# Moving one inner product and five instruction orders in a float32 decoder layer

## The chip, the cores and the metric

The program runs on one core of a Trainium2 chip. The metric is device time in microseconds (us) of one execution. The core has TensorE (PE in the profile, with its weight loads as PEld), VectorE (DVE), ScalarE (ACT), GpSimd (POOL) and SyncE (SP), which here issues most DMAs. Each engine takes its instructions in order, so where an instruction waits, what is queued behind it on that engine waits too.

## The reference

One layer of a hybrid decoder over 1024 prompt tokens and 8 x 8 sample tokens (1088 columns in all), model width 1024, everything float32:

```
xn   = rmsnorm(x, norm1_g)
q, k, v, glu_a, glu_b, gate_a, gate_b = split(xn @ w_in)
A    = attention(q, k, v; window 128, sinks) @ w_o_attn
B    = silu(layernorm(conv31(glu_a * sigmoid(glu_b)))) @ w_pb
h    = x + (sigmoid(gate_a) * A + sigmoid(gate_b) * B) @ w_out
up   = rmsnorm(h, norm2_g) @ w_up                 # 1024 -> 2 x 2816
gate, val = split(conv3(up))
y    = h + (silu(gate) * val) @ w_down            # 2816 -> 1024
out  = rmsnorm(y, norm_f_g)
```

Caches for attention and for both convolutions are outputs too.

## The kernel before

Activations lie as 128 channels by up to 1088 tokens. A float32 product is made of three matmuls (`mm3`, lines 195 to 197): weights and activations are each split into a rounded high part, cast on ScalarE (`whi`, L176 and L230), and the low rest, subtracted on VectorE (`wlo`, L177 and L231). Results gather in PSUM banks taken in turn from two groups, `mm` and `aux`; a bank can be written again when VectorE or ScalarE has moved its result out, an *eviction*.

The program is recorded in Python order, and a scheduler then places each engine's instructions by priorities. `self.later(n)` lowers a priority, `tc.issue_after(x)` puts what is recorded inside behind x, and `self.plan` hands steps to an agenda that `tick` runs off after so many k-steps.

The stages that matter here, in order of time:

- **Attention projection** (`phase_y`, about 640 to 736 us): eight streams `("o", m)`. `stream` calls `weight(what, ahead)`, which splits the weight of this stream and `ahead` more. Beside it the layer norm of the convolution branch runs from the agenda: VectorE adds eight channel blocks (L563), PE takes their mean (L571).
- **Up projection** (`ffn_up`, to about 1385 us): for each of 22 blocks f, a pair of row blocks (gate and value) is worked in quarters by a scheme with fewer products, Strassen-like. `pair(f)` runs its products n = 0, 1, ... in the order of `seq`, each with two halves j; an eviction of product n is L1713 (an add into `st`) or L1748 (a copy). From f = 4 on, eight times, two neighbouring blocks share one product: a *first* pair (f even) and a *second* (f odd). The shared product is itself split into seven small *inner* products, J11, JT2, J21, JT1, J22, JT3, JT4, of six matmuls each, made by `joint`, while the others, 0 to 5, are the *outer* ones. `JOINT_AFTER` says after which outer product an inner one is made, and `names` in `plan_pair` in which order their weights are prepared. JT3 and JT4 belong to the second pair; JT4's result is added to the gate's `st` (L1703). When a pair's results are there, `finish` convolves them: a first tap on ScalarE (L1400), two steps on VectorE for each of gate and value (L1402), Silu (L1408).
- **Down projection** (`ffn_down`, from about 1385 us): four plain groups, `down(0)` to `down(3)`, and two products of the same kind as above, `product(0)` and `product(1)`. The weights of group 0 are loaded and split in the last pair of the up projection (f = 21, n = 4; a plain pair of seven outer products). `product(0)` multiplies weight tiles `aw` with operands 0 to 20, three for each of its seven products p; an operand's word `bw` is loaded on SP (`words`) and split by ScalarE and VectorE (`operand`). L1904 evicts into H. `hooks[(m, p)]` says what is recorded behind product p of row block m.
- **Final norm**: `down(3)` goes over three chunks of columns; `final` takes the mean of squares on PE (L1969), the root on ScalarE and the reciprocal on VectorE (`rstd`, L356 and L357), scales eight blocks (L1973) and stores them in pairs. `tail` makes the last 128 tokens once more with tokens on the partitions, in two halves of 512 columns, squares them with a sum (L1993), and scales both halves (L2001) when the sum of both is there.

For the first norm of the layer the kernel has another form of the factor: `norm1_factor` makes the mean of squares as single columns (L320), and `norm1_spread` spreads the reciprocal root over 128 partitions with two matmuls for each piece (L339).

## Time and profile before

| | |
|---|---|
| runs | 1646.35, 1645.01, 1646.2 us; median 1646.2 |
| profiled execution | 1644.67 us; its span 1642.8 us; granted TensorE clock 0.999 |
| TensorE busy | 1632.3 us (99%), 11534 matmul records |
| VectorE busy | 1400.3 us (85%), 2595 instructions |
| ScalarE busy | 879.8 us (54%), 1844 instructions |
| GpSimd busy | 282.4 us (17%) |
| DMA | 201.57 MB, mean 123 GB/s |

A row of the timeline has the start and the duration in us, engine, line, operation, output <- inputs, shapes and count, and in brackets the idle time of the engine before it with what ended it. A row of the waits has who waited, for whom, the total, how often, and the longest. A row of the windows has the stretch, its length, the busy time and count of each engine, the granted clock, the DMA engines' busy share and GB/s.

### The profile page before, as it was taken

What the parts mean: (1) busy time and instruction counts of PE and PEld (TensorE: products, weight loads), DVE (VectorE), ACT (ScalarE), POOL (GpSimd) and SP (SyncE); (2) the same over time, 40 slices, a digit from 0 to 9 for tenths busy, and PEclk for the clock granted to TensorE, in tenths of its full rate; (3) what the DMA queues carried; (4) which work ended last, traced back from release to release, by engine and by line L of the source; (5) the groups of instructions that cost most, each with busy time, mean ns of one, the idle gap of its engine ahead of it and who ended that gap; (6) DMA issues with size and microseconds to landing.
All of it is one profiled execution on the core that took longest, in us unless ns stands there. A gap on an engine that the chain in (4) does not pass through costs nothing. (4 is left out here: it accounts for less than half of the span.)

```text
span 1642.8 us, 30190 instructions
## 1 busy us (share of the span) xinstructions
PE 1632.3 (99%) x11534; PEld 1614.9 (98%) x11534; DVE 1400.3 (85%) x2595; ACT 879.8 (54%) x1844; POOL 282.4 (17%) x549
## 2 busy tenths in 40 slices
PE   9999999999999999999999999999999999999998
PEld 9999999999999999999999999999999999999997
DVE  7899979999979996788755999988888877979867
ACT  6424277774488754676532466555555555524322
POOL 0100111222011111111102432333333220000000
PEclk9999999999999999999999999999999999999999
DMA  6221222323121255548763632344444334766423
GB/s 211 85 58 54 64 74 58 106 85 112 44 68 44 91 181 192 184 158 224 189 229 103 201 119 78 118 117 114 115 113 113 96 111 136 256 162 162 110 62 109
DMA packets 104856, 201.57 MB, mean 123 GB/s; under 512 B 25992, under 2 KB 56712, under 8 KB 104696
## 3 DMA queue, kind: packets, MB, share of 16 engines
q1 hardware_dynamic: 81528, 131.60, 26.5%
q0 software_dynamic: 22752, 67.79, 13.8%
q8 instruction: 90, 1.47, 0.4%
q14 instruction: 54, 0.44, 0.1%
q10 hardware_dynamic: 432, 0.27, 0.1%
HBM read 137.55 MB, written 64.03 MB: 123 GB/s over the span
## 5 line engine op out<-in xcount | busy, mean ns | idle before, releaser
L195 PE MATMUL mm<-xh,whi 128*128 128x384 f32 (+1 forms) x904 | 301.2, 333 | 0.0
L196 PE MATMUL mm<-xl,whi 128*128 128x384 f32 (+1 forms) x904 | 295.3, 327 | 0.3 <-DVE xl L282 0.2
L197 PE MATMUL mm<-xh,wlo 128*128 128x384 f32 (+1 forms) x904 | 295.4, 327 | 0.0
L196 PEld LDWEIGHTS mm<-xl,whi 128*128 128x128 f32 x904 | 170.0, 188 | 1.7 <-DVE xl L282 0.9
L195 PEld LDWEIGHTS mm<-xh,whi 128*128 128x128 f32 x904 | 169.8, 188 | 0.7
L197 PEld LDWEIGHTS mm<-xh,wlo 128*128 128x128 f32 x904 | 169.7, 188 | 0.1
L1402 DVE SCALAR_TENSOR_TENSOR acc<-st,fc,acc 128x1104 f32<-128x1104 f32 x88 | 119.8, 1364 | 9.2 <-issue 5.8
L176 ACT CAST whi<-wraw 128x1024 fp32r<-128x1024 f32 (+1 forms) x62 | 59.5, 966 | 66.0 <-PE mm L196 51.7
L197 PE MATMUL mm<-th,wlo 128*128 128x272 f32 x320 | 92.4, 289 | 0.0
L196 PE MATMUL mm<-tl,wlo 128*128 128x272 f32 x320 | 92.3, 289 | 0.0
L195 PE MATMUL mm<-th,wlo 128*128 128x272 f32 x320 | 92.3, 289 | 0.0
L525 DVE SCALAR_TENSOR_TENSOR bt<-u,consts,bt 128x513 f32<-128x513 f32 x120 | 89.8, 749 | 0.7
L525 DVE SCALAR_TENSOR_TENSOR c<-sm,hsum,c 128x512 f32<-128x512 f32 x120 | 89.6, 747 | 0.7
L197 PE MATMUL mm<-mh,wlo 128*128 128x272 f32 (+4 forms) x304 | 89.2, 293 | 0.0
L1748 ACT COPY st<-mm 128x272 f32<-128x272 f32 (+2 forms) x132 | 44.0, 351 | 78.0 <-PE mm L197 78.0
L525 DVE SCALAR_TENSOR_TENSOR c<-u,consts,c 128x512 f32<-128x512 f32 x112 | 83.7, 747 | 0.6
L230 ACT CAST whi<-wraw 128x512 fp32r<-128x512 f32 x76 | 47.3, 623 | 55.9 <-DVE wraw L1598 24.9
L177 DVE TENSOR_TENSOR wlo<-wraw,whi 128x1024 fp32r<-128x1024 f32 (+1 forms) x62 | 69.0, 1117 | 7.0 <-ACT whi L176 6.7
L378 ACT ACTIVATE p<-p,nm 128x257 f32<-128x257 f32 (+1 forms) x128 | 62.3, 490 | 11.9 <-DVE nm L373 11.5
L230 ACT CAST wlo<-wraw 128x512 fp32r<-128x512 f32 x76 | 47.5, 625 | 36.2 <-PE mm L197 24.0
L231 DVE TENSOR_TENSOR whi<-wraw,whi 128x512 fp32r<-128x512 f32 x76 | 52.2, 687 | 16.0 <-ACT whi L230 16.0
L195 PE MATMUL aux<-mh,whi 128*128 128x272 f32 (+4 forms) x216 | 63.9, 296 | 0.0
(707 smaller groups left out, 5788.2 us busy)
## 6 DMA issues: line engine op xcount, KB each, us to landing
wraw<-wall SPq DMA_DIRECT2D x118, 512.0 KB, 3.8
bw<-d_b SPq DMA_DIRECT2D x42, 272.0 KB, 4.0
d_b<-gd POOLq DMA_DIRECT2D x36, 272.0 KB, 4.8
d_b<-acc POOLq DMA_DIRECT2D x24, 272.0 KB, 4.5
ar<-wdn SPq DMA_DIRECT2D x32, 192.0 KB, 3.9
d_g<-acc POOLq DMA_DIRECT2D x10, 544.0 KB, 4.1
ga<-d_ga SPq DMA_DIRECT2D x8, 544.0 KB, 5.1
ct<-d_c SPq DMA_DIRECT2D x8, 544.0 KB, 5.7
```

The lines of the kernel that those rows point to most:

```text
L176: self.cast = self.nc.scalar.copy(h[:, z], r[:, z]).ins
L177: self.nc.vector.tensor_tensor(l[:, z], r[:, z], h[:, z].bitcast(F32), ALU.subtract)
L195: mm(ps, wh, xh, start=first, stop=False, skip_group_check=more)
L196: mm(ps, wh, xl, start=False, stop=False, skip_group_check=more)
L197: self.last_mm = mm(ps, wl, xh, start=False, stop=last, skip_group_check=more).ins
L230: self.cast = self.nc.scalar.copy(h, src).ins
L231: self.low = self.nc.vector.tensor_tensor(l, src, h.bitcast(F32), ALU.subtract).ins
L378: nc.scalar.activation(pt[:, j, lo:width + 1], pt[:, j, lo:width + 1], AF.Exp, bias=nm[:, j:j + 1], scale=-1.0, accum_out=den[:, j:j + 1])
L525: mac = lambda o, x, w: nc.vector.scalar_tensor_tensor(o, x, w, o, ALU.mult, ALU.add)
L1402: nc.vector.scalar_tensor_tensor(acc, st[:, k:k + AW], fw(f, k), acc, ALU.mult, ALU.add)
L1748: (add if second and n == 0 and j == 1 else op)(d, r(banks[bank, j]))
```

## The change

Five edits, none of which alters a result beyond the rounding of the last norm's factor.

1. The inner product JT4 stands behind outer product 4 of the second pair in place of 1, in `JOINT_AFTER` and in `names`.
2. The attention projection's stream `("o", 6)` no longer splits the weight of `("o", 7)` ahead; the agenda does, behind the last add of the layer norm's sum.
3. The weights of group 0 of the down projection are still loaded before product 4 of f = 21, but split behind its eviction.
4. In `product(0)`, words 18 to 20 are loaded behind product 0 as before, and their operands split behind products 1, 2 and 3, one each.
5. For the last chunk of `down(3)`, `final` is not called. `tail` makes the factor with `norm1_factor` in two pieces of one column, spreads it by `spread` into PSUM behind the first weight block of the second half, and the eight scalings read it there. The last 128 tokens: the second half is multiplied by the gains on VectorE while its sum is made, scaled on ScalarE and stored from ScalarE's queue; the first is scaled on VectorE and stored from SP.

```diff
-JOINT_AFTER = ({1: "J11", 2: "JT2", 3: "J21", 4: "JT1", 5: "J22"}, {0: "JT3", 1: "JT4"})
+JOINT_AFTER = ({1: "J11", 2: "JT2", 3: "J21", 4: "JT1", 5: "J22"}, {0: "JT3", 4: "JT4"})
...
+LAST_WEIGHT = 153
+FACTOR_AFTER = 1
...
-PIECES = {384: 3, 320: 4}
+PIECES = {384: 3, 320: 4, 256: 2}
...
-            add(live["red"][:, y * n:y * n + n], part[:, 0, :], part[:, 1, :])
+            self.summed = add(live["red"][:, y * n:y * n + n], part[:, 0, :], part[:, 1, :]).ins
...
-            self.stream(("o", m), xa, ev)
+            self.stream(("o", m), xa, ev, ahead=0 if m == KT - 2 else 1)
+
+        def last_weight():
+            with tc.issue_after(self.summed):
+                self.w_split()
 
         for m in range(KT):
+            if m == KT - 2:
+                self.plan([(self.now + LAST_WEIGHT - m * 3 * KT, last_weight)])
             do_o(m)
...
-                names = ("0", "JT3", "1", "JT4", "2", "3", "4", "5")
+                names = ("0", "JT3", "1", "2", "3", "4", "JT4", "5")
...
                     for _ in self.groups[0]:
                         self.w_load()
-                        self.w_split()
...
-                        (add if second and n == 0 and j == 1 else op)(d, r(banks[bank, j]))
+                        self.evicted = (add if second and n == 0 and j == 1 else op)(d, r(banks[bank, j]))
+                if f == NF - 1 and n == 4:
+                    with tc.issue_after(self.evicted.ins):
+                        for _ in self.groups[0]:
+                            self.w_split()
...
-            if last:
+            if last and c < len(TAIL_CHUNKS) - 1:
                 self.final(H, ssq, o, w)
+        self.last_ssq = ssq
...
-        hooks = {(0, 0): each(first, range(15, 21)), (0, 6): [lambda: self.w_ahead(2)], (1, 3): each(gated, (16,)),
+        hooks = {(0, 0): each(first, range(15, 18)) + each(lambda i: words(0, i), range(18, 21)),
+                 (0, 1): each(first, (18,)), (0, 2): each(first, (19,)), (0, 3): each(first, (20,)),
+                 (0, 6): [lambda: self.w_ahead(2)], (1, 3): each(gated, (16,)),
...
+        y = self.t(ft, [P, DM], "acc")
+        o, n = TAIL_CHUNKS[-1]
+        live = self.norm1_factor(ft, 3, self.last_ssq, self.bank("aux"), n)
...
+                if x == 0 and f == FACTOR_AFTER:
+                    self.final_rows(H, self.spread(live, n), o, n)
...
+        nc.vector.tensor_tensor(y[:, cs], ps, grow[:, cs], ALU.mult)
         nc.scalar.activation(s[:, 3:4], s[:, 1:2], AF.Sqrt, bias=s[:, 2:3], scale=1.0 / DM)
         nc.vector.reciprocal(s[:, 3:4], s[:, 3:4])
-        y = self.t(ft, [P, DM], "acc")
-        for cs, ps in halves:
-            nc.vector.scalar_tensor_tensor(y[:, cs], ps, s[:, 3:4], grow[:, cs], ALU.mult, ALU.mult)
-            nc.sync.dma_start(self.a["o_yt"][:, cs], y[:, cs])
+        nc.scalar.activation(y[:, cs], y[:, cs], AF.Identity, scale=s[:, 3:4])
+        nc.scalar.dma_start(self.a["o_yt"][:, cs], y[:, cs])
+        cs, ps = halves[0]
+        nc.vector.scalar_tensor_tensor(y[:, cs], ps, s[:, 3:4], grow[:, cs], ALU.mult, ALU.mult)
+        nc.sync.dma_start(self.a["o_yt"][:, cs], y[:, cs])
```

`final_rows` is the loop of eight scalings and four stores that stood in `final`; `spread` is the matmul part of `norm1_spread`, and it writes the factor to columns 0 to 255 of its bank and returns them.

What the edits do to the engines' orders is seen at three places. The first is VectorE in a joint second pair, from product 4's first eviction (`mm_11575`) on. Its second half lies in `mm_11588`, the gate's rows in `st_11502` and its convolution in `acc_11780`. Before:

```order
L1713 TENSOR_TENSOR st_11568<-st_11568,mm_11575 128x272
L1598 TENSOR_TENSOR wraw_1357_11420<-wraw_1357_11420,wraw_1356_11418 128x512
L1402 SCALAR_TENSOR_TENSOR acc_11780<-st_11502,fc_10182,acc_11780 128x1104
L1713 TENSOR_TENSOR st_11568<-st_11568,mm_11588 128x208
L1713 TENSOR_TENSOR st_11568<-st_11568,mm_11588 128x8x8
L231 TENSOR_TENSOR wlo_1382_11749<-wraw_1357_11420,wlo_1382_11749 128x512
L1402 SCALAR_TENSOR_TENSOR acc_11780<-st_11502,fc_10182,acc_11780 128x1104
L1598 TENSOR_TENSOR wraw_1357_11420<-wraw_1356_11418,wraw_1357_11420 128x512
L1563 TENSOR_TENSOR wraw_1356_11418<-wraw_1356_11418,wraw_11679 128x256
L231 TENSOR_TENSOR whi_1389_11809<-wraw_1357_11420,whi_1389_11809 128x512
```

The same place now, where product 4's halves are `mm_11572` and `mm_11585`, JT4's bank is `mm_11365`, and L1725, L1715, L1414, L1610, L1575 and L233 are the lines that were L1713, L1703, L1402, L1598, L1563 and L231:

```order
L1725 TENSOR_TENSOR st_11565<-st_11565,mm_11572 128x272
L1610 TENSOR_TENSOR wraw_1357_11420<-wraw_1357_11420,wraw_1356_11418 128x512
L1725 TENSOR_TENSOR st_11565<-st_11565,mm_11585 128x208
L1725 TENSOR_TENSOR st_11565<-st_11565,mm_11585 128x8x8
L233 TENSOR_TENSOR wlo_1382_11749<-wraw_1357_11420,wlo_1382_11749 128x512
L1715 TENSOR_TENSOR st_11502<-st_11502,mm_11365 128x272
L1610 TENSOR_TENSOR wraw_1357_11420<-wraw_1356_11418,wraw_1357_11420 128x512
L1575 TENSOR_TENSOR wraw_1356_11418<-wraw_1356_11418,wraw_11672 128x256
L1414 SCALAR_TENSOR_TENSOR acc_11780<-st_11502,fc_10182,acc_11780 128x1104 x2
L233 TENSOR_TENSOR whi_1389_11809<-wraw_1357_11420,whi_1389_11809 128x512
L1414 SCALAR_TENSOR_TENSOR acc_11787<-st_11565,fc_10182,acc_11787 128x1104
```

JT4's add stands between product 4's evictions and the gate's convolution, and both steps of that convolution stand behind it.

The second place is VectorE in `product(0)`, where `bw_16452` is word 20 and `aw` a weight tile. Before:

```order
L231 TENSOR_TENSOR ml_1857_16444<-bw_16442,ml_1857_16444 128x544
L231 TENSOR_TENSOR mh_1859_16449<-bw_16447,mh_1859_16449 128x544
L1904 TENSOR_TENSOR H_15876<-H_15876,aux_16457 128x272
L1904 TENSOR_TENSOR H_15876<-H_15876,aux_16468 128x272
L231 TENSOR_TENSOR ml_1861_16454<-bw_16452,ml_1861_16454 128x544
L231 TENSOR_TENSOR aw_16479<-ar_1775_16005,aw_16479 128x3x128
L1904 TENSOR_TENSOR H_15876<-H_15876,mm_16411 128x272
L1904 TENSOR_TENSOR H_15876<-H_15876,mm_16422 128x272
```

Now (L1920 was L1904, and words 18, 19 and 20 are `bw_16442`, `bw_16444` and `bw_16446`):

```order
L1920 TENSOR_TENSOR H_15876<-H_15876,aux_16448 128x272
L233 TENSOR_TENSOR ml_1861_16470<-bw_16442,ml_1861_16470 128x544
L1920 TENSOR_TENSOR H_15876<-H_15876,aux_16459 128x272
L233 TENSOR_TENSOR aw_16473<-ar_1775_16005,aw_16473 128x3x128
L1920 TENSOR_TENSOR H_15876<-H_15876,mm_16411 128x272
L233 TENSOR_TENSOR mh_1863_16496<-bw_16444,mh_1863_16496 128x544
L1920 TENSOR_TENSOR H_15876<-H_15876,mm_16422 128x272
L233 TENSOR_TENSOR aw_16499<-ar_1776_16007,aw_16499 128x3x128
L233 TENSOR_TENSOR ml_1869_16530<-bw_16446,ml_1869_16530 128x544
```

The three words' splits stand between the evictions, and word 20's behind both evictions of the next `mm` pair.

The third is PE at the end of the program; `mm_18696` and `mm_18716` are the two halves of the last 128 tokens. Before:

```order
L1969 MATMUL aux_18679<-fssq_18544,mean_79 128x256
L195 MATMUL mm_18696<-mh_2106_18144,mh_2103_18117 128x512
L196 MATMUL mm_18696<-ml_2107_18145,mh_2103_18117 128x512
L197 MATMUL mm_18696<-mh_2106_18144,ml_2104_18118 128x512
L195 MATMUL mm_18716<-whi_2065_17881,mh_2078_17989 128x512
L196 MATMUL mm_18716<-wlo_2066_17882,mh_2078_17989 128x512
```

Now (L197 to L199 were L195 to L197, L322 was L320 and L340 was L339):

```order
L322 MATMUL aux_18681<-mean_79,fssq_18544 128x1 x2
L197 MATMUL mm_18691<-mh_2106_18144,mh_2103_18117 128x512
L198 MATMUL mm_18691<-ml_2107_18145,mh_2103_18117 128x512
L199 MATMUL mm_18691<-mh_2106_18144,ml_2104_18118 128x512
L197 MATMUL mm_18727<-whi_2065_17881,mh_2078_17989 128x512
L340 MATMUL aux_18681<-identr_80,rowsh_2166_18685 128x128
L340 MATMUL aux_18681<-identr_80,rowsl_2167_18686 128x128
L340 MATMUL aux_18681<-identr_80,rowsh_2166_18685 128x128
L340 MATMUL aux_18681<-identr_80,rowsl_2167_18686 128x128
L198 MATMUL mm_18727<-wlo_2066_17882,mh_2078_17989 128x512
```

One matmul of 256 columns has become two of one column, and four of 128 columns stand inside the second half.

More of the change, by code (lines that the diff above doesn't have):

```diff
@@ L312, in norm1_chain, with norm1_factor @@
         return last
-    def norm1_factor(self, pp, c, sq, ps):
+    def norm1_factor(self, pp, c, sq, ps, n=None):
         nc = self.nc
-        n = CHUNKS[c][1]
+        n = n or CHUNKS[c][1]
         m = PIECES[n]
@@ L328, in norm1_factor, with spread @@
         return ps, h, l
-    def norm1_spread(self, pp, c, live):
+    def spread(self, live, n):
         nc = self.nc
-        n = CHUNKS[c][1]
         m = PIECES[n]
@@ L340, in norm1_spread @@
                                  start=x is h, stop=x is l)
+        return ps[:, :n]
+    def norm1_spread(self, pp, c, live):
+        n = CHUNKS[c][1]
+        ps = self.spread(live, n)
         rstd = self.t(pp, [P, 384], f"rstd{min(c, 1)}")
-        nc.scalar.copy(rstd[:, :n], ps[:, :n])
+        self.nc.scalar.copy(rstd[:, :n], ps)
         return rstd
@@ L1970, in final, with final_rows @@
         self.rstd(ssq[:, :n], ps[:, :n])
+        self.final_rows(H, ssq[:, :n], o, n)
+    def final_rows(self, H, rstd, o, n):
+        nc = self.nc
         for k in range(KT):
             hs = H[:, k, o:o + n]
-            nc.vector.scalar_tensor_tensor(hs, hs, self.c("gf", k), ssq[:, :n], ALU.mult, ALU.mult)
+            nc.vector.scalar_tensor_tensor(hs, hs, self.c("gf", k), rstd, ALU.mult, ALU.mult)
             if k % 2:
```

## The prediction

> **What bounds the kernel now.** The page's first part comes first.
>
> ```profile
> span 1642.8 us, 30190 instructions
> PE 1632.3 (99%) x11534; PEld 1614.9 (98%) x11534; DVE 1400.3 (85%) x2595; ACT 879.8 (54%) x1844; POOL 282.4 (17%) x549
> ```
>
> TensorE is busy nearly all the time, so only two things can shorten the run: a place where its next matmul starts late, and the stretch behind its last one. The profiled execution took 1644.67 us, 1.9 us more than its span and 1.5 us under the median of the three runs, 1646.2 us. I sum on the profiled execution and carry the difference over to the median. A difference of 0.2% is 3.3 us here, about what a measurement of this kernel can tell from no change.
>
> Next, the view of the waits on PE, which says who makes matmuls late. These two rows name the engine and line that the change moves.
>
> ```profile
> PE mm L195 <- DVE H L1904: 1.0, 1, 1.0
> PE mm L195 <- DVE st L1713: 0.4, 1, 0.4
> ```
>
> They understate it, since modelled matmul ends hide short waits. The sizes are therefore read from the timeline, from start to start.
>
> **Part 1: JT4 between products 4 and 5.** Three stretches of the timeline, PE and VectorE at the first joint second pair, then PE at the last of eight (f = 4, 6 to 18):
>
> ```profile
> 1046.93 0.29 PE L195 MATMUL mm<-th,whi 128*128 128x272 f32 x1
> ...
> 1048.44 0.28 PE L195 MATMUL mm<-mh,wlo 128*128 128x272 f32 x1
> 1048.66 0.39 PE L195 MATMUL mm<-th,whi 128*128 128x272 f32 x1
> 1048.89 0.28 PE L196 MATMUL mm<-tl,whi 128*128 128x272 f32 x1
> ...
> 1046.83 1.36 DVE L1402 SCALAR_TENSOR_TENSOR acc<-st,fc,acc 128x1104 f32<-128x1104 f32 x1
> 1048.11 0.49 DVE L1713 TENSOR_TENSOR st<-st,mm 128x208 f32<-128x208 f32 x2
> ...
> 1340.60 0.28 PE L195 MATMUL mm<-mh,wlo 128*128 128x272 f32 x1
> 1340.82 0.39 PE L195 MATMUL mm<-th,whi 128*128 128x272 f32 x1
> 1341.05 0.29 PE L196 MATMUL mm<-tl,whi 128*128 128x272 f32 x1
> ```
>
> Twelve matmuls of product 5's first half run from 1046.93 to 1048.44, a pitch of 0.126 us. Its second half needs the bank of product 4's second half, which ended just before 1046.93, but the eviction L1713 stands behind a convolution step L1402 and starts at 1048.11. So the matmul after 1048.44 comes at 1048.66 instead of 1048.57, and the one after that 0.23 later instead of 0.126: 0.09 + 0.10 = 0.19 to 0.20 us. At 1340.60 it is the same 0.22 and 0.23. Eight times 0.195 is **1.56 us**.
>
> After, six matmuls of JT4 (6 x 0.126 = 0.76 us) stand between the two products and both L1402 of the gate stand behind the eviction, which can start when its matmuls end, near 1047.1. The wait is then over more than 1 us before it matters. JT4's matmuls are moved, not added: PE work 0. What is late next: ScalarE's first tap of the gate now waits for JT4's add, and the gate's two L1402 with it, so VectorE meets the next pair later. There the nearest deadline is JT2, whose matmul reuses the bank that VectorE clears of J11:
>
> ```profile
> 1058.16 0.43 DVE L1703 TENSOR_TENSOR st<-st,mm 128x272 f32<-128x272 f32 x1
> 1059.97 0.29 PE L195 MATMUL mm<-mh,s 128*128 128x272 f32 x1
> ```
>
> J11 is cleared at 1058.59, 1.38 us ahead. By laying the new order over these durations I find VectorE 0.5 to 0.7 us late there, which leaves about 0.7. On POOL a store changes places with a small operation; no queue that PE waits for is behind it. Bounds: -1.57 to 0, and above it the slower rival; I take -1.56.
>
> **Part 2: down projection's first weights behind product 4's eviction (f = 21).** Timeline of VectorE and PE:
>
> ```profile
> 1380.83 1.23 DVE L177 TENSOR_TENSOR ml<-wraw,mh 128x1024 fp32r<-128x1024 f32 x1 [3.07 <-ACT mh L176]
> 1383.11 0.50 DVE L1713 TENSOR_TENSOR st<-st,mm 128x208 f32<-128x208 f32 x2
> ...
> 1382.96 0.29 PE L197 MATMUL mm<-th,whi 128*128 128x272 f32 x1
> 1383.66 0.39 PE L195 MATMUL mm<-th,whi 128*128 128x272 f32 x1 [0.41 <-DVE st L1713]
> 1383.89 0.29 PE L196 MATMUL mm<-tl,whi 128*128 128x272 f32 x1
> ```
>
> VectorE stands 3.07 us before a weight split whose cast is late, with the eviction of a finished product behind it (f = 21 is no joint pair: its two last products lie between). PE loses 0.70 - 0.126 = 0.57 and then 0.23 - 0.126 = 0.10: **0.67 us**. After, the eviction goes first and the splits, at the same time as now, end no later and hold up nothing before the down projection, which has the twelve matmuls from 1383.66 on (1.5 us) ahead of it. I take -0.67; bounds -0.67 and 0.
>
> **Part 3: product(0)'s operands 18 to 20 split one at a time.** Timeline of VectorE and PE:
>
> ```profile
> 1441.55 0.72 DVE L231 TENSOR_TENSOR ml<-bw,ml 128x544 fp32r<-128x544 f32 x1 [1.65 <-ACT ml L230]
> 1442.66 0.78 DVE L1904 TENSOR_TENSOR H<-H,mm 128x272 f32<-128x272 f32 x2
> ...
> 1441.89 0.28 PE L197 MATMUL aux<-e,aw 128*128 128x272 f32 x1
> 1443.15 0.39 PE L195 MATMUL mm<-e,aw 128*128 128x272 f32 x1 [0.98 <-DVE H L1904]
> 1443.38 0.29 PE L196 MATMUL mm<-e,aw 128*128 128x272 f32 x1
> ```
>
> VectorE waits for word 20, and the eviction L1904 stands behind it. PE loses 1.26 - 0.126 = 1.13 and 0.23 - 0.126 = 0.10: **1.24 us**. After, that eviction and the next weight tile stand ahead of word 20's split. Operands 18 to 20 belong to the last of seven products, two products of 18 matmuls (2.3 us each) further on, so the split itself, no later than now, has room. On SP two loads change places. I take -1.24; bounds -1.24 and, if word 20 holds up the following eviction by as much, 0.
>
> **Part 4: attention projection's last weight.** Only VectorE's order changes: the split (o,7) stands behind the three layer-norm adds, not before. Timeline of PE:
>
> ```profile
> 719.11 0.34 PE L197 MATMUL mm<-q,wlo 128*128 128x384 f32 x1
> 719.29 0.62 PE L571 MATMUL aux<-sm,mean 128*128 128x272 f32 x2
> ```
>
> The matmul that needs the adds starts 0.18 us after its neighbour, the ordinary distance: the adds are just in time. Nothing is gained; the split is wanted only when (o,7) starts. I take 0; bounds 0 and, if it came late by its own length, 1.2 us (the 1.23 of part 2's L177).
>
> **Part 5: final norm and the end.** Four groups of rows: matmuls of one column and the spreading matmuls where the kernel uses them already (timeline, PE), the mean matmul that goes, the last operations, and the windows' rates of the stores.
>
> ```profile
> 24.64 0.72 PE L320 MATMUL aux<-mean,sq 128*128 128x1 f32 x6
> 25.23 0.42 PE L197 MATMUL aux<-xh,q 128*128 128x384 f32 x1
> ...
> 40.69 0.22 PE L339 MATMUL aux<-identr,rowsh 128*128 128x128 f32 x1
> 41.31 0.39 PE L195 MATMUL mm<-xh,whix 128*128 128x384 f32 x1
> ...
> 1631.29 0.59 PE L1969 MATMUL aux<-fssq,mean 128*128 128x256 f32 x2
> 1631.95 0.40 PE L196 MATMUL mm<-ml,mh 128*128 128x512 f32 x1
> 1632.18 0.39 PE L197 MATMUL mm<-mh,ml 128*128 128x512 f32 x1
> ...
> 1636.29 0.60 ACT L1993 ACTIVATE st<-mm 128x512 f32<-128x512 f32 x1 [2.60 <-PE mm L197]
> 1637.64 1.41 DVE L2001 SCALAR_TENSOR_TENSOR acc<-mm,tsum,grow 128x512 f32<-128x512 f32 x2
> 1638.41 1.00 SPq L2002 DMA_DIRECT2D o_yt<-acc  x2
> ...
> 1639.75:1640.00 0.25, 0.00 (x0) 0.00 (x0) 0.00 (x0) 0.00 (x0) 0.00 (x0) 1.00 1.04 385
> 1640.50:1640.75 0.25, 0.00 (x0) 0.00 (x0) 0.00 (x0) 0.00 (x0) 0.00 (x0) 0.50 0.63 230
> ```
>
> On PE, L1969 costs 0.66 from its start to the second matmul behind it, less one pitch of 0.23: 0.43 us go. Two pieces of one column are four passes at 0.59 / 6 = 0.098, 0.39, and about 0.1 of restart behind them as behind the other waits: +0.5. Spreading is four matmuls at 0.62 / 6 = 0.103, 0.41, and 0.05 to 0.1 behind: +0.5. PE's last matmul, the last Square (1636.29) and the last reciprocal come 0.5 to 0.6 later, for no work that the end waits for. The eight norm operations start earlier, which frees VectorE but moves no end.
>
> The trace charges 0.098 us for a one-column pass. The Trainium skill, "TensorE: Matmul & The Clock Gate", section "Wait — 56ns, not 53.3ns?", puts the floor of a small matmul at about 25 ns from start to start; by that, an estimate, the four would cost 0.1 and the sum would be 0.3 us lower. The measured row decides.
>
> What is won back: now the two halves are scaled one behind the other on VectorE, 0.7 each, and the second store leaves at 1639.05 (1637.64 + 1.41). After, ScalarE and VectorE scale a half each at once, and both leave together, 0.7 earlier less the 0.55 of PE: about 1638.85 to 1638.95. But they also transfer together. Now the second store's 262 KB (128 x 512 x 4 bytes) end by 1640.75, and at 385 GB/s they took 0.68, so the first byte moved 1.0 us after the issue. After: 1638.9 + 1.0 + 524 KB at 385 GB/s (1.36) = 1641.2, **+0.45 us**. Bounds: the stores do not slow each other and PE adds 0.1 only, -0.6; PE adds 0.7 and the rate is nearer 300 GB/s, +1.0.
>
> That one engine's queue does not hide the other's transfer is the Trainium skill's rule too ("DMA: Bandwidth & Descriptors", section "Issuing engines are not separate DMA queues": all issuers share the same 16 engines). It speaks against this edit. Without it the second store would end at 1638.9 + 1.0 + 0.68 = 1640.6, and part 5 would be -0.15. No run here has two stores in two queues at the end.
>
> **The sum.** -1.56 - 0.67 - 1.24 + 0 + 0.45 = -3.0 us. The profiled execution would go from 1644.7 to 1641.7, the median from 1646.2 to **1643.2 us**, -0.18%, just inside the 0.2%.
>
> **The rivals.**
> - *The end is no dearer.* One-column passes are cheap or the stores overlap; part 5 is about -0.2 and the sum -3.7: 1642.5. For it: the second store's wait behind the first half is real. Against it: the rows of L320. Chance 0.16.
> - *A wait takes the place of part 1.* VectorE is in order and 85% busy; the delayed taps make another eviction late by the same 0.2. Parts 2, 3 and 5 remain: -1.5, 1644.7. For it: the eight joint pairs leave VectorE hardly any idle time. Against it: the 0.7 us left at JT2. Chance 0.10.
> - *The delayed taps stop PE (slower).* The gate's two L1402, 1.28 from start to start, both land ahead of J11's clearing instead of half of one. VectorE is then 2.56 late against the 1.38 of room; PE waits 1.18 and restarts in 0.1, in eight pairs 10.2. With the -3.0 of the forecast that is +7.2: 1653.4 (a lateness of 1.38 is where it begins; 2.1 makes the whole slower by 0.2%). Chance 0.09.
> - *The change does not do it.* Word 20 or the late cast still stands ahead of an eviction (ScalarE's order is in part unchanged), part 3 and 2 give nothing and part 5 costs: -1.1, 1645.1. Chance 0.05.
>
> **How the numbers follow.** The forecast has 0.60. Its own range is 1642.3 to 1644.4, from part 5's bounds and half of part 1. The range 1641.0 to 1645.6 adds the first, second and last rivals and the scatter of the runs shown, 1645.01 to 1646.35; it leaves out the slower one and the corners. Faster by over 0.2% (under 1642.9): a little under half of the forecast, 0.28, and nearly all of the first rival, 0.15: 0.43. Slower by over 0.2%: 0.09. Within: the rest, 0.48.
>
> **What would show it.** Right: the PE rows after product 5's first half keep 0.126 us at all eight pairs, and the waits on DVE st and DVE H are gone from PE's list; no row of more than 0.05 us takes their place near JT2; the last Square starts 0.5 us later against the last matmul group than now; the two last stores are issued within 0.2 us of each other and end together. Wrong: new waits of PE on L1703's or L1402's successors in the pairs, a matmul waiting for a weight split at the start of the down projection or at (o,7), or an end that comes earlier than 1.7 us after the last store's issue.

## The result, and the profile after

The changed kernel takes 1642.44 us (median of 19 runs, 1641.55 to 1644.54), the kernel before, beside it, 1645.75 (19 runs, 1644.34 to 1648.72). The ratio is 0.9979, with a 95% interval of 0.9972 to 0.9986: 3.3 us faster. Forecast were 3.0 us, from 1646.2 to 1643.2. The profiled execution took 1641.73 us against 1644.67, 2.94 less; its span is the first line here, with the engines' line of the page below it:

```profile
span 1639.9 us, 30209 instructions
PE 1631.1 (99%) x11540; PEld 1615.2 (98%) x11540; DVE 1401.3 (85%) x2597; ACT 880.5 (54%) x1845; POOL 262.7 (16%) x549
```

The view of PE's waits has lost its rows for `H` and `st`; a new one of 0.3 has come (on L1178, near 757 us; the rows on `warm` and `pth` belong to the first stages and stood in the list of before too):

```profile
PE mm L662 <- DVE warm L655: 1.1, 1, 1.1
PE aux L429 <- ACT pth L232: 0.8, 1, 0.8
PE mm L197 <- DVE ml L1178: 0.3, 1, 0.3
```

**Part 1.** Timeline of the changed kernel at the first joint second pair, PE and then VectorE:

```profile
1047.33 0.29 PE L199 MATMUL mm<-ml,s 128*128 128x272 f32 x1
1047.46 0.29 PE L197 MATMUL mm<-th,whi 128*128 128x272 f32 x1
...
1048.85 0.29 PE L199 MATMUL mm<-th,whi 128*128 128x272 f32 x1
1048.97 0.29 PE L197 MATMUL mm<-th,whi 128*128 128x272 f32 x1
...
1060.31 0.29 PE L197 MATMUL mm<-mh,s 128*128 128x272 f32 x1
...
1046.89 0.50 DVE L1725 TENSOR_TENSOR st<-st,mm 128x208 f32<-128x208 f32 x2
...
1048.29 0.43 DVE L1715 TENSOR_TENSOR st<-st,mm 128x272 f32<-128x272 f32 x1
...
1050.15 2.77 DVE L1414 SCALAR_TENSOR_TENSOR acc<-st,fc,acc 128x1104 f32<-128x1104 f32 x2 [0.37 <-ACT acc L1412]
...
1058.28 0.43 DVE L1715 TENSOR_TENSOR st<-st,mm 128x272 f32<-128x272 f32 x1
```

The six matmuls of JT4 end at 1047.46, product 5's first half takes 12 times 0.126 from there, and its second half follows at 1048.97 without a wait. The eviction that had started at 1048.11 starts at 1046.89. J11 is cleared at 1058.71, 1.60 before JT2 needs its bank at 1060.31.

**Parts 2 and 3 (edits 3 and 4).** Timeline of PE and VectorE at f = 21 and in `product(0)`:

```profile
1381.99 0.29 PE L199 MATMUL mm<-th,whi 128*128 128x272 f32 x1
1382.12 0.29 PE L197 MATMUL mm<-th,whi 128*128 128x272 f32 x1
1382.25 0.29 PE L198 MATMUL mm<-tl,whi 128*128 128x272 f32 x1
...
1377.80 0.51 DVE L1725 TENSOR_TENSOR st<-st,mm 128x208 f32<-128x208 f32 x2 [1.00 <-PE mm L199]
1378.21 1.22 DVE L179 TENSOR_TENSOR whi<-wraw,wlo 128x1024 fp32r<-128x1024 f32 x1
...
1440.25 0.28 PE L199 MATMUL aux<-e,aw 128*128 128x272 f32 x1
1440.37 0.29 PE L197 MATMUL mm<-e,aw 128*128 128x272 f32 x1
1440.49 0.29 PE L198 MATMUL mm<-e,aw 128*128 128x272 f32 x1
...
1437.18 0.44 DVE L1920 TENSOR_TENSOR H<-H,mm 128x272 f32<-128x272 f32 x1
```

The steps of 0.70 and 0.23 at f = 21, and of 1.26 and 0.23 in `product(0)`, are all 0.12 to 0.13 now. The first eviction waits for PE alone; the second stands behind a weight tile's split and starts 3.2 before PE takes up that group of banks again (1437.18 and 1440.37). Both go ahead of the splits that had held them up.

**Part 5.** Timeline of the last operations, and the windows around the last stores of after and then of before (the last two columns are the DMA engines' busy share and GB/s):

```profile
1628.14 0.50 PE L322 MATMUL aux<-mean,fssq 128*128 128x1 f32 x4
...
1628.51 0.48 PE L197 MATMUL mm<-mh,mh 128*128 128x512 f32 x1
...
1633.68 0.60 ACT L2020 ACTIVATE st<-mm 128x512 f32<-128x512 f32 x1 [3.19 <-PE mm L199]
1634.40 0.69 DVE L2024 TENSOR_TENSOR acc<-mm,grow 128x512 f32<-128x512 f32 x1 [0.99 <-ACT st L2020]
1635.01 0.15 DVE L2026 RECIPROCAL tsum<-tsum 128x1 f32<-128x1 f32 x1
1635.20 0.72 ACT L2027 ACTIVATE acc<-acc,tsum 128x512 f32<-128x512 f32 x1 [0.50 <-DVE tsum L2026]
1635.20 0.75 DVE L2030 SCALAR_TENSOR_TENSOR acc<-mm,tsum,grow 128x512 f32<-128x512 f32 x1
1635.95 0.38 ACTq L2028 DMA_DIRECT2D o_yt<-acc  x1
1635.98 0.34 SPq L2031 DMA_DIRECT2D o_yt<-acc  x1
```

```profile
1636.00:1636.50 0.50, 0.00 (x0) 0.00 (x0) 0.00 (x0) 0.00 (x0) 0.00 (x0) 1.00 0.00 0
1636.50:1637.00 0.50, 0.00 (x0) 0.00 (x0) 0.00 (x0) 0.00 (x0) 0.00 (x0) 1.00 0.35 135
1637.00:1637.50 0.50, 0.00 (x0) 0.00 (x0) 0.00 (x0) 0.00 (x0) 0.00 (x0) 1.00 1.02 389
...
1638.00:1638.50 0.50, 0.00 (x0) 0.00 (x0) 0.00 (x0) 0.00 (x0) 0.00 (x0) 0.50 0.43 152
```

```profile
1638.50:1639.00 0.50, 0.00 (x0) 0.00 (x0) 0.50 (x1) 0.00 (x0) 0.00 (x0) 1.00 0.98 350
1639.00:1639.50 0.50, 0.00 (x0) 0.00 (x0) 0.04 (x1) 0.00 (x0) 0.00 (x0) 1.00 0.90 309
1639.50:1640.00 0.50, 0.00 (x0) 0.00 (x0) 0.00 (x0) 0.00 (x0) 0.00 (x0) 1.00 1.04 387
```

From the start of the mean of squares (1631.29 before, 1628.14 now) to the last Square it is 5.00 before and 5.54 now, and to the end of the span 11.51 and 11.76. Before, the DMA engines never rest: the last half's stores run straight behind those of the eight row blocks. Now they are idle or all but idle (a share of 0.06 and then 0.00) from 1635.25 to 1636.75, and then move both halves together. The spans are given to 0.1, so the times to the end are good to about 0.05.

### The profile page after: what moved, and what is told of

Its sections match the earlier page's. It is cut to its first block, busy times and chain, and to the rows that moved or that the text cites. A ratio compares the mean times of both kernels' runs of the same rounds, so it can differ in the third digit from the quotient of the medians.

```text
span 1639.9 us, 30209 instructions
## 1 busy us (share of the span) xinstructions
PE 1631.1 (99%) x11540; PEld 1615.2 (98%) x11540; DVE 1401.3 (85%) x2597; ACT 880.5 (54%) x1845; POOL 262.7 (16%) x549
## 4 chain that ended last, share of the span: by engine, by line
PE 87%; DVE 7%; ACT 3%; DMA 2%; issue 1%; ACTq 0%; SPq 0%; DVEq 0%; POOLq 0%
PE mm L197 20%; PE mm L198 20%; PE mm L199 20%; PE aux L199 6%; PE aux L198 6%; PE aux L197 6%; PE aux L417 1%; DVE c L531 1%; ACT ct L611 1%; PE aux L429 1%; PE aux L430 1%; PE aux L407 1%; PE aux L408 1%; DVE bt L531 1%; DMA ct<-d_c 1%
## 5 line engine op out<-in xcount | busy, mean ns | idle before, releaser
L197 PE MATMUL mm<-xh,whi 128*128 128x384 f32 (+1 forms) x904 | 301.3, 333 | 0.0
L199 PE MATMUL mm<-xh,wlo 128*128 128x384 f32 (+1 forms) x904 | 295.4, 327 | 0.0
L197 PEld LDWEIGHTS mm<-xh,whi 128*128 128x128 f32 x904 | 169.9, 188 | 0.7
L199 PEld LDWEIGHTS mm<-xh,wlo 128*128 128x128 f32 x904 | 169.7, 188 | 0.1
L1414 DVE SCALAR_TENSOR_TENSOR acc<-st,fc,acc 128x1104 f32<-128x1104 f32 x88 | 119.7, 1363 | 12.2 <-issue 6.7
L199 PE MATMUL mm<-th,wlo 128*128 128x272 f32 x320 | 92.4, 289 | 0.0
L197 PE MATMUL mm<-th,wlo 128*128 128x272 f32 x320 | 92.4, 289 | 0.0
L199 PE MATMUL mm<-mh,wlo 128*128 128x272 f32 (+4 forms) x304 | 89.2, 293 | 0.0
L1412 ACT ACTIVATE acc<-st,fc 128x1104 f32<-128x1104 f32 x44 | 57.6, 1314 | 14.5 <-DVE st L1715 11.9
L197 PE MATMUL aux<-mh,whi 128*128 128x272 f32 (+4 forms) x216 | 63.9, 296 | 0.0
```

Of the source, the lines that this page charges most:

```text
L197: mm(ps, wh, xh, start=first, stop=False, skip_group_check=more)
L199: self.last_mm = mm(ps, wl, xh, start=False, stop=last, skip_group_check=more).ins
L1412: nc.scalar.activation(acc, st[:, 0:AW], AF.Identity, bias=fb(f), scale=fw(f, 0))
L1414: nc.vector.scalar_tensor_tensor(acc, st[:, k:k + AW], fw(f, k), acc, ALU.mult, ALU.add)
```

## The experiments

Times of runs of one kernel scatter by some 2 to 4 us, so the parts are read from the traces: the start of the same matmul on PE is compared with the kernel before, and a stretch of the program is worth what this difference grows by. Edit 2 acts between 700 and 740 us; the joint pairs are edit 1, f = 21 is edit 3, the words are edit 4. The last column is the time from the mean of squares to the end of the span.

| run | us | 700 to 740 | 740 to 762 | joint pairs | f = 21 | words | tail |
|---|---|---|---|---|---|---|---|
| before | 1644.67 | | | | | | 11.51 |
| after | 1641.73 | +0.03 | +0.71 | -1.50 | -0.67 | -1.24 | 11.76 |
| jt4_last | 1642.05 | +0.10 | +0.35 | -1.50 | -0.67 | -1.24 | 11.78 |
| jt4_three | 1643.01 | +1.48 | +0.42 | -1.64 | -0.68 | -1.24 | 11.73 |
| jt4_two | 1643.51 | +1.36 | +0.21 | -0.94 | -0.67 | -1.24 | 11.76 |
| only_last_weight | 1646.26 | +1.51 | +0.27 | +0.02 | +0.75 | -1.00 | 11.53 |
| split_and_words | 1642.63 | +0.24 | +0.37 | -0.02 | -0.67 | -1.24 | 11.49 |
| old_mean_new_halves | 1641.08 | +0.02 | +0.30 | -1.50 | -0.67 | -1.24 | 11.66 |
| new_mean_old_halves | 1643.01 | +1.11 | +0.34 | -1.49 | -0.67 | -1.24 | 11.48 |
| one_queue | 1641.90 | +0.13 | +0.37 | -1.50 | -0.67 | -1.24 | 11.75 |
| quarters | 1641.78 | +0.03 | +0.03 | -1.50 | -0.67 | -1.24 | 12.65 |
| end_alone | 1645.52 | +1.62 | +0.55 | 0.00 | -0.02 | -1.12 | 11.96 |

All are single profiled executions. One loss is in no column: new_mean_old_halves loses 0.73 more near 955 us, where PE waits for a weight split (L1463), and no other kernel does. The runs fall into three groups.

**JT4's place (part 1).** The first two kernels move JT4 on from its new place, the third goes between old and new.

```diff
-JOINT_AFTER = (..., {0: "JT3", 4: "JT4"})
+JOINT_AFTER = (..., {0: "JT3", 5: "JT4"})   # jt4_last
+JOINT_AFTER = (..., {0: "JT3", 3: "JT4"})   # jt4_three
+JOINT_AFTER = (..., {0: "JT3", 2: "JT4"})   # jt4_two
```

(`names` follows.) For jt4_last the expectation was:

> The changed kernel with JT4 behind outer product 5 instead of 4: no inner product stands between products 4 and 5 any more, but VectorE's order keeps both L1402 steps of the gate behind product 4's eviction. Theory (the wait of 0.19 us in each joint second pair came from the convolution step ahead of the eviction): the eviction starts near the end of product 4, a good 1 us before its bank is wanted, so the eight waits stay away and the stretch of the joint pairs is within 0.2 us of the changed kernel. Rival (JT4's 0.76 us of matmuls between the products are what covers the wait): 0.09 + 0.10 us come back at each of eight pairs, +1.5 us. A second rival: JT4's bank comes free later and the next pair's first matmuls wait, up to 0.5 us a pair, +4 us.

It came out so: -1.50 and no wait in the eight pairs, with no matmuls of JT4 between products 4 and 5. The cover is not needed. For jt4_three:

> The changed kernel with JT4 behind outer product 3 instead of 4: JT4 is still moved away from product 1, and one step of the gate's convolution stands ahead of product 4's second eviction again, as in the kernel before. Theory (VectorE's order decides): the eight waits are back with about 0.19 us each, the stretch of the joint pairs is 1.5 us longer than in the changed kernel. Rival (it is enough that JT4 is later than product 1): no waits, the stretch as in the changed kernel.

This failed. One step of the convolution does stand ahead of the eviction, and yet the stretch gives -1.64. Timeline of VectorE in before, where JT4's add is the first row, and in jt4_three, where it is the L1715:

```profile
1039.10 0.43 DVE L1703 TENSOR_TENSOR st<-st,mm 128x272 f32<-128x272 f32 x1
...
1045.27 0.69 DVE L231 TENSOR_TENSOR whi<-wraw,whi 128x512 fp32r<-128x512 f32 x1 [0.40 <-ACT whi L230]
```

```profile
1046.25 0.43 DVE L1715 TENSOR_TENSOR st<-st,mm 128x272 f32<-128x272 f32 x1
1046.74 0.69 DVE L233 TENSOR_TENSOR whi<-wraw,whi 128x512 fp32r<-128x512 f32 x1
...
1048.42 1.36 DVE L1414 SCALAR_TENSOR_TENSOR acc<-st,fc,acc 128x1104 f32<-128x1104 f32 x1
1049.70 0.50 DVE L1725 TENSOR_TENSOR st<-st,mm 128x208 f32<-128x208 f32 x2
```

PE is 1.97 later in jt4_three at this place (most of it its loss near 720 us, below). Counted from PE, the split of `whi` starts at 1044.77 there and at 1045.27 before, and the eviction at 1047.73 and 1048.11. In before JT4's add stands in a stretch in which VectorE has next to no idle time, and then VectorE idles 0.40 for a cast. In jt4_three the add stands in that idle time, the cast and all behind it come earlier, and the eviction is 0.38 earlier, twice the 0.19 that PE lost. So a third theory: not what stands directly ahead of the eviction, but how late VectorE is when it gets there, and behind product 2 the add should still make it late:

> JT4 behind outer product 2, the rest as in the changed kernel. Theory: VectorE works without a gap for 12 us ahead of the late eviction, up to an idle stretch of 0.40 us where it waits for a cast; JT4's add (0.43) makes the eviction late as long as it stands in that full stretch. Behind product 2 it still does, so the 0.19 at each of eight pairs comes back: the joint stretch changes by 0 against before and the run is 1.5 slower than the changed kernel. If any place later than product 1 were enough, the stretch shows -1.5 as with JT4 behind product 3.

```profile
1043.32 0.43 DVE L1715 TENSOR_TENSOR st<-st,mm 128x272 f32<-128x272 f32 x1
...
1046.92 0.69 DVE L233 TENSOR_TENSOR whi<-wraw,whi 128x512 fp32r<-128x512 f32 x1 [0.40 <-ACT whi L232]
...
1049.76 0.50 DVE L1725 TENSOR_TENSOR st<-st,mm 128x208 f32<-128x208 f32 x2
```

Half right. The idle 0.40 is back and so is a part of the wait, but only a part: -0.94 instead of 0 and instead of -1.5. Counted from PE (1.74 later here) the eviction starts at 1048.02, 0.09 earlier than before. The eight pairs are not alike: in the first six PE still loses 0.10 each (no wait is left, only the slow step of 0.23 instead of 0.126 behind it), in the last two nothing. Together, counted from the eviction's start to the matmul that takes its bank: 0.46 before (to where that matmul would stand without the wait), with a loss of 0.19 a pair; 0.55 in those six pairs, with 0.10; 0.68 in the last two, 0.65 to 0.95 in jt4_three, 1.31 in jt4_last and 2.08 in the changed kernel, with none. The lateness sets the price, about tenth for tenth; the changed kernel wins 1.6 where 0.2 were enough.

**Edits 2 to 4.** Edit 2 alone, and edits 3 and 4 alone, on the kernel before:

```diff
+            self.stream(("o", m), xa, ev, ahead=0 if m == KT - 2 else 1)   # only_last_weight
...
+                    with tc.issue_after(self.evicted.ins):                  # split_and_words
+                        for _ in self.groups[0]:
+                            self.w_split()
```

> The kernel before with the edit of the attention projection's last weight alone. In the profile of the changed kernel the stretch from 740 to 760 us took 0.72 us longer than before, with a cast waiting 1.2 us for a weight load instead of 0.7. Theory (chance of one load's landing, the edit is neutral): the stretch is within 0.3 us of the kernel before, and where it is not, the load was issued at the same time and landed later; the whole is 1644 to 1646. Rival (the weight load that the moved split releases goes out 2.4 us later and pushes the later loads): the same +0.5 to +0.8 us again, and a new wait of PE on DVE ml near 757.

> The kernel before with two edits alone: the down projection's first weights split behind product 4's eviction at f = 21, and operands 18 to 20 of product(0) split one by one. Theory: PE's waits on DVE st near 1383 and on DVE H near 1442 are gone and nothing takes their place, -0.67 and -1.24 us, together -1.9 us against the kernel before. Rival (ScalarE's order is partly unchanged, so a late cast holds up another eviction): half of it or less, with a new wait of PE within 10 us behind either place.

The second came out to the hundredth: -0.67 and -1.24, and no new wait. The first came out between 740 and 762 us (+0.27), but showed +1.51 near 720 us, where PE waits for the layer norm's sum. That looked like a cost of edit 2, but the end alone, whose program is that of before up to the last 20 us, has it too:

```profile
720.47 0.73 PE L577 MATMUL aux<-sm,mean 128*128 128x272 f32 x2 [1.33 <-DVE sm L569]
```

> The new end alone, on the kernel before. The tail from the mean of squares to the end is 11.76, 0.25 longer than before, with the last Square at 5.54; the joint stretch, f = 21 and the words change by 0, and no wait of PE near 720 or 760 us is new: about 1645.9 beside 1645.7.

Of the eleven profiled executions with edit 2 (those of the table, and old_end and serial_quarters below) four lose 1.1 to 1.5 us there, of the three without it one. It is scatter of a load: VectorE's work on the second half of that layer norm's input waits for a DMA, first in before, then in end_alone:

```profile
698.17 0.72 DVE L563 TENSOR_TENSOR u<-ct 128x544 f32<-128x544 f32 x1 [0.87 <-DMA ct<-d_c]
```

```profile
699.47 0.73 DVE L569 TENSOR_TENSOR u<-ct 128x544 f32<-128x544 f32 x1 [2.06 <-DMA ct<-d_c]
```

That load took 7.0 to 7.2 us from issue to landing in the five executions with the loss and 5.5 to 5.8 in the other nine. The norm's later steps carry the delay on: ScalarE's Square (L596) starts at 717.52 in end_alone against 716.22 in before (L590). Why the load lands late was not settled. The 0.03 to 0.71 near 750 us are taken for scatter as well: a cast there waits 0.17 to 1.25 for a weight load in all runs, and the runs without edit 2 show 0.37 and 0.55. Edit 2 itself does bring the sum forward: its last add starts 2.38 behind that Square in all eleven executions with the edit and 2.60 in all three without. These 0.22 count only where PE waits for the sum; between before and after they did not.

The last column but one holds one more thing. In the two runs that came 1.8 late from 720 us without edit 4, the wait for word 20 was nearly gone (-1.12 and -1.00): the word landed 0.7 and 1.7 later than before, while PE came to it 1.84 and 2.70 later. A loss ahead of such a wait can be paid back by it, but need not be: in only_last_weight the wait at f = 21 grew by 0.75, since its weight load was issued 1.8 later, as PE was, but landed 2.5 later.

**The end (part 5).** Four kernels are the changed one with a piece of its end undone or altered:

```diff
-            if last and c < len(TAIL_CHUNKS) - 1:
+            if last:                     # old_mean_new_halves: factor and scalings as before
...
+        for cs, ps in halves:            # new_mean_old_halves: halves one behind the other, as before
+            nc.vector.scalar_tensor_tensor(y[:, cs], ps, s[:, 3:4], grow[:, cs], ALU.mult, ALU.mult)
+            nc.sync.dma_start(self.a["o_yt"][:, cs], y[:, cs])
...
-        nc.scalar.dma_start(self.a["o_yt"][:, cs], y[:, cs])
+        nc.sync.dma_start(self.a["o_yt"][:, cs], y[:, cs])      # one_queue
...
+        for x in range(2):               # quarters: each half in two pieces of 256 columns
```

> The changed kernel with the last chunk's factor made as before (mean matmul, root and reciprocal of 128 x 256 in SBUF), the last 128 tokens as changed. Times are counted from the start of the mean's matmul (1631.29 before, 1628.14 changed): before, the last Square comes at 5.00, the second store at 7.78, the end of the span at 11.51; changed, 5.54, 7.84, 11.76. Theory (one-column and spreading matmuls cost PE 0.5; VectorE is then the bound, since its eight scalings end at 6.2 as before and the multiply stands behind them): Square at 5.0, stores at 7.6 to 7.7, end 11.5 to 11.7. Rival (the new form's 0.5 us of PE is all there is to it): everything behind the Square 0.54 earlier, stores at 7.3, end at 11.2.

> The changed kernel with the last 128 tokens scaled and stored as before (both halves on VectorE one behind the other, both stores from SP), the factor as changed. From the start of the mean's matmul, as in the run beside it. Theory: Square at 5.54, reciprocal right behind the root at 6.6, stores at 7.6 and 8.3, end 3.73 behind the second, 12.0: 0.25 us worse than changed, 0.5 worse than before. Rival (two stores that leave together share the engines so that nothing is won by leaving together): end 11.7 to 11.8 as changed.

> The changed kernel with the second half's store issued from SP too, in front of the first half's. Theory (all stores share the same 16 engines, and the end is set by 524 KB behind the first byte): the first store leaves as now, the second one issue of 0.34 us later, both end within 0.15 us of the changed kernel (11.76 from the mean's matmul to the end of the span). Rival (two queues move more than one): the end is 0.3 us or more later.

> The changed kernel with each half of the last 128 tokens scaled and stored in two pieces of 256 columns, two on ScalarE, two on VectorE, so that the first bytes can move about 0.35 us earlier. Theory (behind the last scaling the stores' transfer bounds the end): first stores at 7.45 instead of 7.82 from the mean's matmul, the last at 7.9, end 11.4 to 11.5, 0.3 us earlier than changed. Rival (the end is bound by the time from the last issue to the landing, 3.9 us): end 11.8 or later.

old_mean_new_halves came out as expected (Square 5.00, stores 7.64 and 7.67, end 11.66). The other three follow the table.

| kernel | last Square | stores issued | bytes move from about | tail |
|---|---|---|---|---|
| before | 5.00 | 7.13, 7.79 | without a pause | 11.51 |
| after | 5.54 | 7.80, 7.83 | 8.7 | 11.76 |
| old_mean_new_halves | 5.00 | 7.64, 7.67 | 8.5 | 11.66 |
| new_mean_old_halves | 5.52 | 7.55, 8.21 | 8.4 | 11.48 |
| one_queue | 5.54 | 7.80, 8.24 | 8.6 | 11.75 |
| quarters | 5.51 | 7.54, 7.57, 8.02, 9.73 | 8.4 | 12.65 |

Times are in us from the mean of squares. new_mean_old_halves went against its expectation of 12.0: with the second store leaving 0.4 later than in after, the end is 0.28 earlier. Its windows show why:

```profile
1638.00:1638.50 0.50, 0.00 (x0) 0.00 (x0) 0.00 (x0) 0.00 (x0) 0.00 (x0) 1.00 0.76 291
1638.50:1639.00 0.50, 0.00 (x0) 0.00 (x0) 0.00 (x0) 0.00 (x0) 0.00 (x0) 1.00 1.05 385
1639.00:1639.50 0.50, 0.00 (x0) 0.00 (x0) 0.00 (x0) 0.00 (x0) 0.00 (x0) 0.94 0.94 365
```

The transfer of one half (0.68) is as long as the scaling of one (0.66 from start to start), so two halves one behind the other keep the DMA engines full from the first store on. What counts between these two is when the first half leaves: 7.55 there, 7.80 in after. one_queue gave 11.75, as expected: the second store leaves 0.41 later and the end does not move. That agrees with the Trainium skill, "DMA: Bandwidth & Descriptors", section "Issuing engines are not separate DMA queues", by which DMAs started from different engines run on the same 16 DMA engines. quarters failed by 1 us. Timeline of its two queues:

```profile
1634.90 2.54 SPq L2035 DMA_DIRECT2D o_yt<-acc  x2
1634.92 0.84 ACTq L2030 DMA_DIRECT2D o_yt<-acc  x2
```

SP's second store is issued 1.8 after its data are there (scaled by 7.91, issued at 9.73). It waits for the DMA semaphore that ScalarE's first store uses as well, and the view of SP's waits has a landing of the same tensor for it:

```profile
SPq L2035 <- DMA o_yt<-acc: 1.8, 1, 1.8
```

So it waited for that store to land; a kernel with a semaphore for each store was not run. The last two kernels ask whether the end can be bettered: parts 1 to 4 with the end of before (old_end), and the changed kernel with four pieces one behind the other (serial_quarters).

```diff
+        for x, a, b in ((0, 0, 256), (0, 256, 512), (1, 0, 256), (1, 256, 512)):   # serial_quarters
+            z = slice(512 * x + a, 512 * x + b)
+            nc.vector.scalar_tensor_tensor(y[:, z], halves[x][1][:, a:b], s[:, 3:4], grow[:, z], ALU.mult, ALU.mult)
+            nc.sync.dma_start(self.a["o_yt"][:, z], y[:, z])
```

> Parts 1 to 4 with the end of the kernel before. If the end costs what the traces so far show (11.51 us from the last mean of squares to the end of the span before, 11.76 now), this kernel is 0.25 us faster than the changed one: the joint stretch -1.50, f = 21 -0.67, the words -1.24, together -3.4 against before, about 1642.3 beside 1645.7. If the new end were a gain that the single traces hide, it is slower than the changed kernel.

> The changed kernel, but its last 128 tokens are scaled in four pieces of 256 columns, one behind the other on VectorE, each stored from SP as it is done. Theory: the 524 KB move at the DMA engines' rate from the first store's first byte on, so the end hangs on when the first piece leaves. First store 7.2 us behind the mean of squares, first byte 0.85 later, 524 KB at about 340 GB/s (the rate of pieces of 1 KB) 1.54, the end 1.7 behind the last byte: 11.3, 0.45 earlier than the changed kernel and 0.2 earlier than with two serial halves. Rival: the end follows the last store's issue, which is at 8.3, by the 3.3 to 3.9 seen so far: 11.6 to 12.2. A second rival: a store of a quarter waits for an earlier one, as one did when four left from two queues, and the end is past 12.5.

old_end has a tail of 11.53, 0.23 shorter than after's, as expected, and 1642.6 us (11 runs) beside 1644.77 of before: ratio 0.9986, interval 0.9977 to 0.9995. serial_quarters has a tail of 11.71 instead of 11.3, and 1641.94 us (11 runs): 0.9977, interval 0.9968 to 0.9986. Its stores leave at 7.29, 7.73, 8.21 and 8.70, and the bytes start at 8.1 as reckoned, but they then move at no more than 270 GB/s, not at 340:

```profile
1637.00:1637.50 0.50, 0.00 (x0) 0.00 (x0) 0.03 (x1) 0.00 (x0) 0.00 (x0) 0.50 0.81 266
1637.50:1638.00 0.50, 0.00 (x0) 0.00 (x0) 0.00 (x0) 0.00 (x0) 0.00 (x0) 0.50 0.82 270
```

A piece leaves every 0.47 and 131 KB at 340 GB/s last 0.39, so the engines pause between pieces. The intervals of both kernels overlap with the changed one's (0.9972 to 0.9986): no end tried here is faster by more than the runs can tell, and none of these versions is shown to beat the changed kernel.

One more difference between the kernels is no wait. Between about 1603 and 1616 us the matmuls of 352 columns follow each other at 0.160 us in after, where before has 0.163, which gains 0.24 to 0.27 in all. The three jt4 kernels, old_mean_new_halves, new_mean_old_halves, quarters and end_alone have it too; old_end, one_queue, serial_quarters, only_last_weight and split_and_words have not. Every kernel that has it holds a piece of edit 5, but two with a piece of edit 5 lack it. In end_alone every engine's order is that of before up to the mean of squares, so the order of instructions does not make it; the cause is open. Were it put down to edit 5, that edit would cost about nothing in after.

## Why the prediction was right, point by point

- **Part 1** was forecast at -1.56 and measured -1.50. The sum held, and the reason given for it, that the eviction no longer stands behind the convolution step, is enough but more than was needed: jt4_three leaves that step ahead of the eviction and loses nothing. The step *what is late next* was off: I found VectorE 0.5 to 0.7 late at JT2 with 0.7 us left; 1.60 are left, more than the 1.38 of before. With it the slower rival lost its ground, and so did the wait that takes part 1's place.
- **Parts 2 and 3**: -0.67 and -1.24, both as forecast, and the same in every run that had both edits and in split_and_words alone. The rule used, the step at the wait less the pitch, plus 0.10 for the slow matmul behind it, is exact here, because it prices the waits of the very execution that the others are compared with. In another execution the wait has another size: at f = 21 it cost 0.67, 0.65 and 1.42 in the three without edit 3, in `product(0)` 1.24, 0.12 and 0.24 in the three without edit 4. It depends on when a load lands against PE, so -1.9 is not shown to be what the two edits gain on average.
- **Part 4** (edit 2) at 0: right between these two executions, since PE did not wait for the sum in either. That nothing is gained is not right in general: the sum comes 0.22 earlier, which is worth up to that much where PE waits for it.
- **Part 5** was forecast at +0.45 and measured +0.25 (11.73 to 11.78 in four runs with this end, and 11.96 once). PE's share, 0.5 to 0.6 later, was 0.54. Two steps were off and partly cancel. The stores leave 7.80 behind the mean of squares and not 7.55 to 7.65, because the multiplication by the gains, which I had not put on the path, waits by a semaphore for ScalarE's Square of the same bank (1634.40), and the reciprocal stands behind it (6.87; 6.57 in new_mean_old_halves, which has no multiplication). That two engines on one bank are made to wait for each other, ScalarE and VectorE too, stands in the Trainium skill, "PSUM — Partial Sum Buffer", section "PSUM bank collisions raise a hardware error"; the trace agrees, with VectorE idle 0.99 until ScalarE was through. And the transfer counted 1.0 from issue to the first byte, which took about 0.85. The forecast *what is won back* (the halves 0.7 earlier) is wrong as a mechanism: the halves side by side lose 0.28 against one behind the other (11.76 and 11.48), about the 0.30 by which the multiplication delays the reciprocal; halves side by side without that multiplication were not run. What is won back is in the other half of the edit: the row blocks' stores are all but over about 7.0 behind the mean of squares instead of 8.0, their last packets 7.6 instead of 8.5. In before the last packet of the two halves ends 0.32 behind the first 98% of their packets (9.82 and 9.50), in new_mean_old_halves 0.06 (9.89 and 9.83). That pays for the 0.54 on PE (11.48 against 11.51); that late packets of the row blocks are what holds up the last packets in before is inferred, not tested.
- **The sum**: -1.50 - 0.67 - 1.24 + 0.25 = -3.16, against -3.0. On top the trace has -0.18 up to 740 us, +0.71 near 750 and -0.26 near 1610, which come and go among the kernels; the execution is 2.94 faster. That this comes so near to the 3.0 is in part luck: the 0.27 of these three, which the sum did not have, and the 0.20 by which it had part 5 too dear nearly cancel. The -0.26 is also a way to a shorter run that the prediction's opening (late matmuls and the end alone) leaves out. *The change does not do it* fell with parts 2 and 3, *the end is no dearer* with the tail of 11.76.
- The one-column passes took 0.37 / 4 = 0.093 apiece (1628.14 to 1628.51), as the row of L320 had it (0.098) and nearly four times the 25 ns of the Trainium skill's "TensorE: Matmul & The Clock Gate", section "Wait — 56ns, not 53.3ns?". The measured row was the right one to take.

## What to carry to other kernels

A wait of a busy TensorE for an in-order engine is priced from start to start on both sides of it, and it is removed either by moving what stands ahead of the eviction or by making the evicting engine a few tenths less late; its size in one trace can be that of one load's landing. Look for an idle gap behind a full stretch, and put the movable work into the gap. At the end of a program it matters when the first of the last bytes leaves, if the DMA engines then run without a pause (serial_quarters left earliest, 7.29, and paused between pieces): two halves whose scaling takes as long as their transfer should then gain nothing from being scaled side by side. And before a single trace's wait is put down to an edit, see whether runs without that edit have it too.

## What the runs showed of the hardware

- Two 262 KB stores leaving within 0.03 us of each other from two queues move at 389 GB/s together, no faster than the two that left 0.66 apart from one queue before (385 to 393): the end is the same from one queue (11.75) and from two (11.76).
- Four 131 KB stores from one queue, 0.47 apart, moved at 266 to 270 GB/s.
- A matmul of 128x272 that came just in time behind an eviction, or late, was followed by a step of 0.23 us instead of 0.126.
- A load of the same tensor, issued at the same place of the program, landed in 5.5 to 5.8 us in nine executions and in 7.0 to 7.2 in five.
- Matmuls of 352 columns at the same place of the program followed each other at 0.163 us in six kernels and at 0.160 in eight, at a granted clock of 1.00 in before and after; the cause is open.
